# Second token blocks of an expert in whole fp32 products on 64 rows, in a hybrid decoder block on one core

## The chip, the core and the metric

The kernel runs on one core of a Trainium2 chip. The metric is the device time of one execution in microseconds. Five engines work side by side and order themselves by semaphores: TensorE (PE for its products, PEld for its weight loads), VectorE (DVE), ScalarE (ACT), GpSimd (POOL) and SyncE (SP). Transfers run on 16 DMA engines; SyncE issues most of them here, GpSimd the gathers and scatters of rows.

## The reference

One layer over 512 tokens of width 1024: a Mamba-2 mixer and a pooling mixer, merged and projected, and then a mixture of 64 experts, of which each token takes 8. Only the last part is touched by the change. In the routed experts (cut; the sorting into blocks is told in a comment):

```python
scores = jax.nn.sigmoid(uf @ w_router)            # 512 x 64
# 4 of 8 groups of experts, then the best 8 experts of these, for each token
wts = wts / jnp.sum(wts, axis=-1, keepdims=True) * ROUTED_SCALE
# the tokens of an expert, in blocks of 128:
xb = u_pad[toks]                                   # rows x 1024
hid = jax.nn.silu(xb @ we_gate[e]) * (xb @ we_up[e])   # 1024 x 256 each
y = (hid @ we_down[e]) * ws[:, None]               # 256 x 1024
# y is added to the rows of its tokens
```

An expert with up to 128 tokens has one block, one with up to 256 has two. All is float32.

## The kernel before

The mixers take about the first half of the time and the 64 experts, in a loop that is written out, the second. An expert's weights come in three tiles of 1 MB: `gu[e][0]` and `gu[e][1]` (gate and up, for one half of the 1024 inputs each) and `dn[e]`. Eight such raw tiles go round (`raw_tile`, L924); `load(e + 2)` (L1280) asks SyncE for the weights of the expert after the next, and a tile is written again when all its readers, in the code of every arm, are through.

There are two ways to compute a block.

- The heavy way splits both operands into a high and a low part of a rounded type and makes three products for each whole one (`mm3`, L59). Weights are split by ScalarE and VectorE (`split`, L43) into `wh`, `wl` or the pairs kept apart; rows are transposed by TensorE (`turn_in`), copied by ScalarE and subtracted by VectorE (`turn_out`, L902). A block of up to 128 rows takes 24 products of 512 columns for gate and up (`gate_up_mm`, L957) and 12 for the down projection (`down`, L1033).
- The light way serves experts with up to `LIGHT` = 64 tokens. It takes whole float32 products straight from the raw tiles: the gate products write partitions 0 to 63 of a PSUM tile, the up products partitions 64 to 127 (`gate_up_light`, L970), and so do the two halves of the down projection (`down_light`, L979). The products are copied out (L1185), transposed, and Silu and the multiply come after the transposes on 64 columns (L1224 to L1226).

A branch on the expert's count (`by_count`, L1155) picks one or the other at run time, on each engine by itself. Second blocks, of experts with over 128 tokens (`if_two`, L1165), always go the heavy way, on all 128 rows, though the gather and the scatter are made for 64 or 128 rows by the count (`second`, L1124). Experts with over 256 tokens are finished by a general path after the loop (`rare_blocks`, L1294), that runs if `k.rare` (L818) is set.

The order of work is written out by hand. In the turn of expert e (L1234 on) TensorE makes: the products of e (L1243); if e has a second block, its gate and up products (`second_products`); the transposes of the rows of e + 1; if e + 1 has a second block, the transposes of these rows (`next_second`); the down projection of e - 1 (`downs(e - 1)`, L1274); the transposes of the hidden rows of e (`hidden_turned`, L1275, that is L1008 with `ht`); and, if e has a second block, its hidden rows' transposes and its down projection (`second_down`, L1276). ScalarE and VectorE go through the same list with their own parts. GpSimd scatters the rows of e - 1, then those of the second block of e, and gathers for e + 2 at the start of the turn.

Second blocks use `k.xT` (the buffer of the other parity) for their rows, `hid1`, `k.hx[2]` for the hidden rows, the rows' tile `k.xg[2]` for the result, and the split weights of the first block.

Of the kernel before, what the change touches and what calls it, by code (L numbers as in the profile page):

```python
# [11 lines left out]
F32 = mybir.dt.float32  # L12
F32R = mybir.dt.float32r
BF16 = mybir.dt.bfloat16
I32 = mybir.dt.int32
AF = mybir.ActivationFunctionType
ALU = mybir.AluOpType
# [4 lines left out]
P = 128  # L22
# [734 lines left out]
def route(k, rp, lg):  # L757
# [59 lines left out]
    k.rare = mp.tile([P, 1], I32, name="rare")  # L817
    nc.vector.tensor_scalar(k.rare, cm, 2.0 * P, None, op0=ALU.is_gt)  # L818

# [98 lines left out]


def split_pair(hp, lp):  # L920
    return (hp.tile([P, 2048], F32R, name="wh", tag="wh"), lp.tile([P, 2048], F32R, name="wl", tag="wl"))
# [57 lines left out]
def down_light(k, x, unit, y, w):  # L979

    nc = k.nc
    ps = k.yo.tile([P, 512], F32, name="yo", tag="yo")
    for j in range(2):
        for n in range(2):
            nc.tensor.matmul(ps[n * LIGHT:(n + 1) * LIGHT, :], x[:, j, :], unit.raw[:, j * D + n * 512:j * D + n * 512 + 512],  # L985
                             start=j == 0, stop=j == 1)
    for n in range(2):
        nc.scalar.activation(y[:LIGHT, n * 512:(n + 1) * 512], ps[n * LIGHT:(n + 1) * LIGHT, :], AF.Copy, scale=w[:LIGHT])  # L988


# [21 lines left out]
def hidden_out(k, ps, hx):  # L1012
    nc = k.nc
    nc.scalar.copy(hx[0], ps)
    nc.vector.tensor_sub(hx[1], ps, hx[0].bitcast(F32))
# [59 lines left out]
def experts(k, shared):  # L1075
# [48 lines left out]
    def second(e, move):  # L1124
        n = count(e)
        with tc.If(n > P):
            with tc.If(n <= P + 64) as some:
                move(64)
            with some.Else():
                move(P)  # L1130

# [89 lines left out]
    def hidden_turned(e, hid):  # L1221
        ps = hidden_in(k, hid)

        def light():  # L1224
            nc.scalar.activation(k.hT, ps[:, :, :LIGHT], AF.Silu)
            nc.vector.tensor_mul(k.hT, k.hT, ps[:, :, LIGHT:])  # L1226

        by_count(e, both, light, lambda: hidden_out(k, ps, k.hx[e % 2]))

    with tc.manual_schedule():  # L1230
        fetch_over(0)
        fetch_over(1)
        if_two(0, lambda: turn(k, k.xg[3], k.xT[1]))
        for e in range(E):  # L1234
# [16 lines left out]
            def second_products():  # L1251
                gate_act(k, gate_up_mm(k, k.xT[(e + 1) % 2], gu[e]), hid1)
                turns()
# [5 lines left out]
            def next_second():  # L1259
                index_part(0)  # L1260
                turn(k, k.xg[3 + (e + 1) % 2], k.xT[e % 2])

            def second_down():
                ps = turn_tiles(k)[0].rearrange("p q t -> p (q t)")[:, :2 * P].rearrange("p (j t) -> p j t", j=2)
                hidden_in(k, hid1, ps)
                index_part(1)
                hidden_out(k, ps, k.hx[2])
                for n in range(2):
                    down(k, k.hx[2], dn[e], n, k.xg[2], idx[e][1][:, 1:2])

# [23 lines left out]
def rare_blocks(k):  # L1294
# [3 lines left out]
    with tc.If(r):  # L1298
# [4 lines left out]
        with tc.For_i(0, E, 1) as e:  # L1303
# [9 lines left out]
            split_bf16(k, k.wp, pk[:, NT:], [vv[:, :, 2 + i] for i in range(3)])  # L1313
            for b in (2, 3):
                pm = k.wp.tile([P, NT], F32, name="pmb", bufs=2)
                nc.vector.tensor_scalar(pm, pk[:, :NT], -128.0 * b, None, op0=ALU.add)
                idx = slot_rows(k, slot_onehot(k, pm, 1, nc.vector), vv, 1)
                whole_block(k, gather(k, idx, 0, k.xg[3]), idx, 0, gu, dn, k.xT[0], k.hx[0])
# [46 lines left out]
def block_kernel(ctx, tc, a, out):  # L1365
# [54 lines left out]
    with ExitStack() as p2:  # L1420
# [5 lines left out]
        k.hT = k.wp.tile([P, 2, LIGHT], F32, name="hT")  # L1426
        k.hx = [tuple(k.wp.tile([P, 2, P], F32R, name=f"h{n}{i}") for n in "hl") for i in range(3)]
        spx = ExitStack()
# [46 lines left out]
```

## Time and profile before

| | before |
|---|---|
| median of 3 runs | 1675.88 us |
| lowest and highest | 1669.54 and 1677.01 us |
| the profiled execution | 1673.0 us, its span 1671.3 us |
| granted TensorE clock, mean | 0.947 of full speed |
| busy: PE, PEld, DVE, ACT, POOL | 88%, 69%, 61%, 45%, 22% |
| moved by DMA | 340 MB, mean 204 GB/s |

The busy shares are over the whole span. The span is what lies between the first and the last instruction in the profile; the execution's time has 1.7 us around it. PE is counted busy from a product's start to its modelled end, and products overlap, so that the starts tell more than the lengths.

### The profile page before, as it was taken

What the parts mean: (1) busy time and instruction counts of PE and PEld (TensorE: products, weight loads), DVE (VectorE), ACT (ScalarE), POOL (GpSimd) and SP (SyncE); (2) the same over time, 40 slices, a digit from 0 to 9 for tenths busy, and PEclk for the clock granted to TensorE, in tenths of its full rate; (3) what the DMA queues carried; (4) which work ended last, traced back from release to release, by engine and by line L of the source; (5) the groups of instructions that cost most, each with busy time, mean ns of one, the idle gap of its engine ahead of it and who ended that gap; (6) DMA issues with size and microseconds to landing.
All of it is one profiled execution on the core that took longest, in us unless ns stands there. A gap on an engine that the chain in (4) does not pass through costs nothing. (4 is left out here: it accounts for less than half of the span.)

```text
span 1671.3 us, 25992 instructions
## 1 busy us (share of the span) xinstructions
PE 1475.4 (88%) x8084; PEld 1156.2 (69%) x8084; DVE 1011.8 (61%) x1744; ACT 745.2 (45%) x1027; POOL 370.3 (22%) x312
## 2 busy tenths in 40 slices
PE   5999999999999999999898888898798888887970
PEld 5888788788888778888675666566576665665640
DVE  6889778778877974558743354545436453355326
ACT  3465546454434223325544455444536454355332
POOL 5201101002010111220122322322324222221226
PEclk7999999999999999999999999899899989898995
DMA  9442433243333236236738778958889999898974
GB/s 288 122 126 76 138 102 121 76 126 101 107 105 117 82 114 233 87 115 227 294 113 285 252 235 289 329 189 258 282 251 313 324 329 318 287 325 273 297 288 151
DMA packets 152127, 340.32 MB, mean 204 GB/s; under 512 B 15816, under 2 KB 94832, under 8 KB 142272
## 3 DMA queue, kind: packets, MB, share of 16 engines
q1 hardware_dynamic: 135888, 294.94, 51.8%
q0 software_dynamic: 15408, 40.23, 9.4%
q8 instruction: 118, 1.93, 0.5%
q10 hardware_dynamic: 576, 2.10, 0.3%
q14 instruction: 137, 1.12, 0.2%
HBM read 314.00 MB, written 31.01 MB: 206 GB/s over the span
## 5 line engine op out<-in xcount | busy, mean ns | idle before, releaser
L46 DVE TENSOR_TENSOR wl<-raw,wh 128x2048 fp32r<-128x2048 f32 x114 | 273.5, 2404 | 100.0 <-ACT wh L45 88.4
L45 ACT CAST wh<-raw 128x2048 fp32r<-128x2048 f32 x114 | 216.6, 1906 | 140.3 <-PE mm L62 65.7
L1044 POOL DMA_INDIRECT Y<-yl,idx x64 | 108.2, 1691 | 481.8 <-ACT yl L988 271.9
L61 PE MATMUL mm<-uh,wh 128*128 128x512 f32 x432 | 171.7, 397 | 1.9 <-ACT zs L285 1.9
L63 PE MATMUL mm<-uh,wl 128*128 128x512 f32 x432 | 170.4, 395 | 0.0
L62 PE MATMUL mm<-ul,wh 128*128 128x512 f32 x432 | 169.8, 393 | 0.0
L899 PE MATMUL xt<-ident,xg 128*128 128x128 f32 x632 | 97.2, 300 | 58.2 <-issue 18.6
L899 PEld LDWEIGHTS xt<-ident,xg 128*128 128x128 f32 x632 | 84.9, 196 | 77.7 <-issue 48.9
L976 PE MATMUL gu<-raw,xf 128*64 128x256 f32 x1056 | 125.9, 387 | 6.1 <-DMA raw<-in_we_up_dram 3.5
L885 POOL DMA_INDIRECT xg<-u2d,idx x75 | 93.5, 1247 | 117.5 <-DVE oh L851 36.4
L46 DVE TENSOR_TENSOR pair<-raw,pair 128x2048 fp32r<-128x2048 f32 x33 | 75.0, 2290 | 58.2 <-ACT pair L45 49.7
L976 PEld LDWEIGHTS gu<-raw,xf 128*64 128x64 f32 x1056 | 77.2, 138 | 42.6 <-issue 7.2
L61 PE MATMUL gu<-wh,xh 128*128 128x512 f32 x256 | 103.1, 403 | 1.0 <-ACT xh L909 0.6
L62 PE MATMUL gu<-wl,xh 128*128 128x512 f32 x256 | 101.9, 398 | 0.7 <-DVEq L1169 0.7
L63 PE MATMUL gu<-wh,xl 128*128 128x512 f32 x256 | 101.3, 396 | 0.0
L1226 DVE TENSOR_TENSOR hT<-hT,ht 128x128 f32<-128x128 f32 x33 | 9.5, 288 | 146.8 <-ACTq L1169 142.5
L61 PEld LDWEIGHTS mm<-uh,wh 128*128 128x128 f32 x432 | 81.6, 189 | 20.4 <-ACT zs L285 2.3
L63 PEld LDWEIGHTS mm<-uh,wl 128*128 128x128 f32 x432 | 81.6, 189 | 17.7 <-issue 0.9
L62 PEld LDWEIGHTS mm<-ul,wh 128*128 128x128 f32 x432 | 81.5, 189 | 16.8 <-issue 0.4
L45 ACT CAST pair<-raw 128x2048 fp32r<-128x2048 f32 x33 | 62.1, 1903 | 61.7 <-DMA raw<-in_we_gate_dram 22.8
L985 PE MATMUL yo<-raw,hT 128*64 128x512 f32 x264 | 75.5, 695 | 3.5 <-DMA raw<-in_we_gate_dram 2.0
L327 DVE SCALAR_TENSOR_TENSOR cv<-mm,cw,cv 128x511 f32<-128x511 f32 (+2 forms) x90 | 66.6, 741 | 2.1 <-ACT cv L324 1.8
(354 smaller groups left out, 3336.8 us busy)
## 6 DMA issues: line engine op xcount, KB each, us to landing
raw<-in_we_gate_dram SPq DMA_DIRECT2D x124, 512.0 KB
raw<-in_we_up_dram SPq DMA_DIRECT2D x124, 512.0 KB
raw<-in_we_down_dram SPq DMA_DIRECT2D x62, 1024.0 KB
raw<-in_w_in_dram SPq DMA_DIRECT2D x27, 1024.0 KB
raw<-in_w_ada_dram SPq DMA_DIRECT2D x16, 1024.0 KB
big<-in_w_ada_dram SPq DMA_DIRECT2D x16, 512.0 KB
raw<-in_w_in_dram SPq DMA_DIRECT2D x16, 512.0 KB
raw<-in_w_br_ssd_dram SPq DMA_DIRECT2D x8, 1024.0 KB
```

The source lines that it names most:

```text
L45: nc.scalar.copy(h, raw)
L46: nc.vector.tensor_sub(l, raw, h.bitcast(F32))
L61: nc.tensor.matmul(out, sh, mh, start=first, stop=False)
L62: nc.tensor.matmul(out, sh, ml, start=False, stop=False)
L63: nc.tensor.matmul(out, sl, mh, start=False, stop=last)
L327: nc.vector.scalar_tensor_tensor(cv[:, sft:], ps[:, :T - sft], k.cw[:, j * 32 + blk:j * 32 + blk + 1], cv[:, sft:], op0=ALU.mult, op1=ALU.add)
L885: k.nc.gpsimd.indirect_dma_start(out=xg[:n], out_offset=None, in_=k.u2d, bounds_check=T - 1, oob_is_err=False, in_offset=bass.IndirectOffs ...
L899: k.nc.tensor.transpose(pv[:, q, :], xv[:, hf * 4 + q, :], k.ident)
L976: nc.tensor.matmul(ps[s * LIGHT:(s + 1) * LIGHT, :256], x[:, kk, :], w[:, s, kk % 4, :], start=kk == 0, stop=kk == NK - 1)
L985: nc.tensor.matmul(ps[n * LIGHT:(n + 1) * LIGHT, :], x[:, j, :], unit.raw[:, j * D + n * 512:j * D + n * 512 + 512], start=j == 0, stop=j ...
L1044: k.nc.gpsimd.indirect_dma_start(out=k.Y[acc], out_offset=bass.IndirectOffsetOnAxis(ap=idx[0][:n, b:b + 1], axis=0), in_=y[:n], in_offset= ...
L1226: nc.vector.tensor_mul(k.hT, k.hT, ps[:, :, LIGHT:])
```

## The change

Second blocks go the light way, on at most 64 rows: their rows are turned into `k.xf` (the light experts' tile) by copies alone (`turn_light`), gate and up are made by `gate_up_light` from the raw tiles and copied out, Silu and the multiply follow the transposes (`act_light`, which is also what light experts use now), and `down_light` writes the result with its two evictions. Gather and scatter of second blocks are always of 64 rows; the question at L1127 goes. The general path starts at over 192 tokens instead of 256, and its blocks at token 192, 320 and 448. The third pair of `k.hx` goes.

```diff
-    nc.vector.tensor_scalar(k.rare, cm, 2.0 * P, None, op0=ALU.is_gt)
+    nc.vector.tensor_scalar(k.rare, cm, float(P + LIGHT), None, op0=ALU.is_gt)
...
+def turn_light(k, src, x):
+
+    halves = turn_tiles(k)
+    turn_in(k, src, halves)
+    for hf, pv in enumerate(halves):
+        k.nc.scalar.copy(x[:, hf * 4:hf * 4 + 4, :], pv[:, :, :LIGHT])
...
+def act_light(k, ps, x):
+
+    k.nc.scalar.activation(x, ps[:, :, :LIGHT], AF.Silu)
+    k.nc.vector.tensor_mul(x, x, ps[:, :, LIGHT:])
...
     def second(e, move):
-        n = count(e)
-        with tc.If(n > P):
-            with tc.If(n <= P + 64) as some:
-                move(64)
-            with some.Else():
-                move(P)
+        with tc.If(count(e) > P):
+            move(LIGHT)
...
-        if_two(0, lambda: turn(k, k.xg[3], k.xT[1]))
+        if_two(0, lambda: turn_light(k, k.xg[3], k.xf))
...
             def second_products():
-                gate_act(k, gate_up_mm(k, k.xT[(e + 1) % 2], gu[e]), hid1)
+                g = k.gu.tile([P, 512], F32, name="gu", tag="gu")
+                gate_up_light(k, k.xf, gu[e], g)
+                nc.scalar.copy(hid1, g[:, :256])
                 turns()
...
             def next_second():
                 index_part(0)
-                turn(k, k.xg[3 + (e + 1) % 2], k.xT[e % 2])
+                turn_light(k, k.xg[3 + (e + 1) % 2], k.xf)
 
             def second_down():
                 ps = turn_tiles(k)[0].rearrange("p q t -> p (q t)")[:, :2 * P].rearrange("p (j t) -> p j t", j=2)
                 hidden_in(k, hid1, ps)
                 index_part(1)
-                hidden_out(k, ps, k.hx[2])
-                for n in range(2):
-                    down(k, k.hx[2], dn[e], n, k.xg[2], idx[e][1][:, 1:2])
+                act_light(k, ps, k.hT)
+                down_light(k, k.hT, dn[e], k.xg[2], idx[e][1][:, 1:2])
...
-            for b in (2, 3):
+            for b in range(3):
                 pm = k.wp.tile([P, NT], F32, name="pmb", bufs=2)
-                nc.vector.tensor_scalar(pm, pk[:, :NT], -128.0 * b, None, op0=ALU.add)
+                nc.vector.tensor_scalar(pm, pk[:, :NT], -float(P + LIGHT + P * b), None, op0=ALU.add)
```

## Rows read from the trace of the kernel before

**Rows 1.** The page: busy share of TensorE, and the DMA engines in 40 slices (tenths)
```profile
PE 1475.4 (88%) x8084; PEld 1156.2 (69%) x8084; DVE 1011.8 (61%) x1744; ACT 745.2 (45%) x1027; POOL 370.3 (22%) x312
DMA  9442433243333236236738778958889999898974
```

**Rows 2.** Branches by source line: TensorE's at L1169, GpSimd's at L1127 (ns: min/median/max)
```profile
L1169 PEldq COMPARE_BRANCH  x225: 65/215/2042, 808.3 to 1620.7; - x113
L1127 POOLq COMPARE_BRANCH  x44: 34/40/41, 809.2 to 1542.6; - x44
```

**Rows 3.** Gate and up products in stretches: us, PE busy (count), clock, DMA share, GB/s
```profile
902.20:916.73 14.53, 11.32 (x48) 1.00 0.73 259
934.79:949.21 14.42, 11.32 (x48) 1.00 0.83 257
...
sum 180.80, PE 124.56; mean PE 11.32
```

**Rows 4.** All of TensorE's products in the same eleven stretches, their sum
```profile
sum 180.80, PE 175.25; mean PE 15.93
```

**Rows 5.** Timeline of TensorE, 908 to 926 us: start, length, instruction, count, idle before
```profile
908.25 0.40 PE L61 MATMUL gu<-wh,xh 128*128 128x512 f32 x1
...
913.80 1.05 PE L899 MATMUL xt<-ident,xg 128*128 128x128 f32 x8
...
914.87 1.94 PE L985 MATMUL yo<-raw,hT 128*64 128x512 f32 x8
916.73 0.51 PE L1008 MATMUL ht<-ident,hid 128*128 128x128 f32 x2
...
918.96 0.51 PE L61 MATMUL yo<-pair,hh 128*128 128x512 f32 x1 [1.39 <-ACT hh L1014]
...
921.65 0.40 PE L63 MATMUL yo<-pair,hl 128*128 128x512 f32 x1
921.98 3.67 PE L976 MATMUL gu<-raw,xf 128*64 128x256 f32 x32
925.58 1.16 PE L899 MATMUL xt<-ident,xg 128*128 128x128 f32 x8
```

**Rows 6.** Timeline of ScalarE in the same stretch
```profile
903.73 0.28 ACT L1225 ACTIVATE hT<-ht 128x128 f32<-128x128 f32 x1
...
914.00 0.39 ACT L998 ACTIVATE hid<-gu 128x256 f32<-128x256 f32 x1 [5.12 <-PE gu L63]
...
916.85 1.38 ACT L988 ACTIVATE yl<-yo,wt 64x512 f32<-64x512 f32 x2 [1.53 <-PE yo L985]
...
918.52 0.38 ACT L1014 CAST hh<-xt 128x256 fp32r<-128x256 f32 x1
...
923.74 1.90 ACT L45 CAST wh<-raw 128x2048 fp32r<-128x2048 f32 x1 [0.91 <-DMA raw<-in_we_up_dram]
```

**Rows 7.** Timeline of VectorE in the same stretch
```profile
904.04 0.29 DVE L1226 TENSOR_TENSOR hT<-hT,ht 128x128 f32<-128x128 f32 x1 [3.39 <-ACTq L1169]
...
918.66 0.42 DVE L1015 TENSOR_TENSOR hl<-ht,hh 128x256 fp32r<-128x256 f32 x1 [3.82 <-ACT hh L1014]
```

**Rows 8.** ScalarE waiting for weights: a timeline row; waits from 834 to 1266 us
```profile
890.91 1.90 ACT L45 CAST wh<-raw 128x2048 fp32r<-128x2048 f32 x1 [3.54 <-DMA raw<-in_we_up_dram]
...
ACT wh L45 <- DMA raw<-in_we_up_dram: 25.3, 10, 5.4
```

**Rows 9.** Timeline of TensorE behind the fifth second block
```profile
991.89 0.48 PE L1008 MATMUL xt<-ident,hid 128*128 128x128 f32 x2 [2.66 <-DVEq L1169]
```

**Rows 10.** Timeline of SyncE's queue: the first and the last transfer of a burst
```profile
916.06 0.33 SPq L946 DMA_DIRECT2D raw<-in_we_gate_dram  x1
...
918.87 0.72 SPq L947 DMA_DIRECT2D raw<-in_we_up_dram  x1
```

**Rows 11.** Engines in the loop's two parts: PE, PEld, DVE, ACT, POOL, clock, DMA, GB/s
```profile
834.00:1266.00 432.00, 377.57 (x2147) 279.41 (x2146) 189.22 (x367) 200.46 (x283) 116.85 (x78) 0.94 0.77 248
1266.00:1628.00 362.00, 302.69 (x1819) 214.27 (x1815) 161.19 (x318) 170.17 (x241) 93.68 (x65) 0.93 0.90 308
```

More of the change, by code (lines that the diff above doesn't have):

```diff
@@ L1222, in hidden_turned @@
         ps = hidden_in(k, hid)
[L1224 to L1228, printed above, removed]
+        by_count(e, both, lambda: act_light(k, ps, k.hT), lambda: hidden_out(k, ps, k.hx[e % 2]))
     with tc.manual_schedule():
@@ L1426, in block_kernel @@
         k.hT = k.wp.tile([P, 2, LIGHT], F32, name="hT")
-        k.hx = [tuple(k.wp.tile([P, 2, P], F32R, name=f"h{n}{i}") for n in "hl") for i in range(3)]
+        k.hx = [tuple(k.wp.tile([P, 2, P], F32R, name=f"h{n}{i}") for n in "hl") for i in range(2)]
         spx = ExitStack()
```

## The prediction

> **What bounds the kernel now.** I read the page first: TensorE is busy for 88% of the span, and the transfers are lighter in the first half of the expert loop than in the second [rows 1]. Then I counted the second blocks. L1169 is every question "has this expert over 128 tokens?"; TensorE's sequencer asks it 192 times (once ahead of the loop, three times in each of 64 turns, less one in the last), and the branch out of a taken arm that has an Else is counted too: 225 - 192 = 33, three for an expert, so 11 experts have a second block. L1127 asks for each of them, once at the gather and once at the scatter, whether 192 tokens suffice: 22 questions. It stands there 44 times, so each of the 22 was followed by the branch that leaves its first arm, and no expert has over 192 tokens [rows 2]. That settles how often the changed path runs, and that the general path stays unused.
>
> For where the 11 blocks lie I cut the loop at the first transpose of an expert's hidden layer (L1008 `ht`), which gives one stretch for each expert e. The products of both blocks of e fall in its own stretch, the second block's down projection at the start of the next. In the 11 stretches the gate and up products keep TensorE busy 11.32 us on average for the two blocks, 5.66 us each [rows 3], and all TensorE work together fills 175.25 of 180.80 us [rows 4]. TensorE has no room there, so a microsecond less of its work is a microsecond less of time, unless a later wait swallows it.
>
> **The change part by part.** I take the stretch of the first block pair that is followed by a light expert, 902 to 926 us, since it shows both ways of computing side by side.
>
> *Gate and up products.* The 24 products of the second block start at 908.25 and the next work at 913.80: 5.55 us, 0.23 each. The light way is in the same view: 32 instructions from 921.98 to the next work at 925.58, 3.60 us [rows 5]. Entering the half-array form costs a little: the last full product before it starts at 921.65, so 0.33 us instead of 0.23, 0.10 more. New cost 3.70, saved 1.85 us a block, 11 x 1.85 = 20.4 us. One rule of the Trainium skill speaks against this: FP8 and Floating Point Precision, section TensorE Precision Notes, counts four passes for true fp32. By that my estimate would be 16 products x 4 x 256 columns / 2.4 GHz = 6.8 us, longer than the 5.55 of today. The row says 3.60, because the two halves (gate to partitions 0 to 63, up to 64 to 127) run side by side. The second such rule, TensorEngine Tiling (Array Packing), section Key Properties, says that changing the tiling mode drains the engine; the trace's price for that is the 0.10 us above, and it is in the sum.
>
> *What follows the products.* ScalarE's Silu and VectorE's multiply on `hid1` give way to one copy; Silu and multiply come back on 64 columns after the transposes. The first pair hid behind TensorE: ScalarE waited 5.12 us for TensorE ahead of it [rows 6]. That is also more than the 1.85 us by which TensorE now comes earlier, so ScalarE doesn't become the end here.
>
> *Turning the second block's rows.* The eight transposes stay. Two ScalarE copies of half the columns replace two copies and two VectorE subtractions. No TensorE wait ends on those subtractions in this view; I cost it at nothing. The cover is the old down projection behind it (1.86 us from 914.87 [rows 5]); it only gets wider.
>
> *Down projection.* 12 products run from 918.96 to 921.98, 3.02 us; the light form takes from 914.87 to 916.73, 1.86, and some 0.11 more for a first product after a wait (the first of the 12 has that too), 1.97 us. Saved 1.05. But the wait ahead of it grows. Today TensorE starts 0.06 us after ScalarE's second copy, at 918.52 + 0.38. In the new form that instruction is the Silu of 64 columns, 0.27 us, and then VectorE's multiply, 0.29, has to follow (904.04, right behind ScalarE's 903.73 + 0.28); VectorE is busy with the first block's subtraction from 918.66 for 0.42 [rows 5 to 7]. So the multiply starts at 919.08, ends at 919.37, and TensorE starts at 919.43, 0.47 later. Where VectorE is free it is 0.27 + 0.03 + 0.29 - 0.38 = 0.21 later. I take 0.43: the net gain is 0.62 us a block. The two evictions stay two of 0.69 (1.38 us for the pair in the light row at 916.85), but both now start after the last product, where today the first is done while the second half is computed. In this stretch ScalarE ends at 919.43 + 1.97 + 1.38 = 922.78 instead of 922.83 (0.91 before the split at 923.74 [rows 6]): nothing gained.
>
> *Which of these 0.62 us survive.* Where a light expert stands between two experts with second blocks (two of the 11), TensorE next waits for the weight split that ScalarE starts after these evictions, so the gain is nothing. Behind three others (the second, seventh and eighth of the eleven) the next heavy expert's first split waits for its weights. Behind the second it begins at 890.91, after 3.54 us of waiting, and those weights were requested in the second pair's own stretch, ahead of the down projection [rows 8]. What comes after the request and before the wait gains nothing. I drop 5 of 11 and keep 6 x 0.62 = 3.7 us. Behind the fifth pair the transposes of the second block's hidden rows already wait 2.66 us on VectorE's queue [rows 9]; I take off 0.3 us of the products' gain for that.
>
> *Weights held longer.* The second block now reads the raw tiles, not their split copies. SyncE's reloading waits for all readers of a tile, in the code of every expert. Its transfers come in bursts: the first waits for the previous expert's down projection (916.06, in TensorE's light run of 914.87), and the others follow to 918.87 [rows 10]. TensorE has passed the second block's products before that projection, so the new readers are done when the burst starts; `dn` is freed by the down projection of the first block, later still. Cost nothing; bounds zero and rival 3.
>
> *POOL, registers, general path.* The nested question at L1127 goes, 22 times some 0.04 us, on an engine that isn't at the end. The threshold in `rare` is one constant. Nothing.
>
> **Sum.** 20.4 + 3.7 - 0.3 = 23.8 us against the profiled execution: 1673.0 - 23.8 = 1649.2. That execution lies 2.9 us under the median of the runs shown, 1675.88, and inside their spread; I forecast 1650, half way to what the median would give.
>
> **The rivals.** 1, the transfers take it back. In the stretches from 834 to 1266 us, which hold ten of the pairs, the DMA engines are busy 0.77 of the time, from 1266 to 1628 us 0.90 [rows 11]. Ten pairs 2 us shorter make 0.77 of 432 into 0.81 of 412 us; on average there is room, but ScalarE already waits 25.3 us for `up` weights in the first part, ten times [rows 8]. If all of the 3.7 and 40% of the 20.4 go into such waits, 12 us stay: 1661. For it: bursts of three transfers in a row and a wait that already exists. Against: the request moves earlier with TensorE, and in the shortened stretches the share is 0.73 and 0.83 in the rows shown [rows 3].
> 2, more than the sum: no longer wait, nothing swallowed, 11 x (1.85 + 1.05) = 31.9 us, 1641. For it: VectorE loses two subtractions a block and a multiply on 256 columns. Against: VectorE's multiply is now on the way to the down products.
> 3, slower: the release of the raw tiles comes later than I read from the code, for all 64 experts. Were the second and third transfer of a burst to wait for the end of the next down projection, 921.98 instead of 916.73, they would be 5.25 us late. In the second half (31 stretches in 362 us, 11.7 each, a tenth of it without transfers) 1.2 us can be late without harm; beyond that each stretch grows, by up to 4.0 us, 31 x 4.0 = 124 us: 1773. Against it: TensorE's order above. It decides from a delay of 1.2 us, and 2 us would make the kernel slower than now (31 x 0.8 = 25).
> 4, it doesn't do what it says: the saved TensorE time is there and the ends don't move, because each stretch ends on ScalarE or VectorE splits; under 8.4 us remain. 5.5 of 180.8 us of idle time in the 11 stretches speak against it [rows 4].
>
> **How the numbers follow.** Forecast, 18 to 30 us saved: 0.60. Rival 1: 0.17. Rival 2: 0.08. Rival 4: 0.10. Rival 3, with the general path: 0.05. The range: 1638 is rival 2 less the runs' spread of 0.2%; 1664 is rival 1 plus it. It leaves out most of rivals 3 and 4, 0.15, and a little at the low end. A measurement of this kernel can tell about 0.5% from no change, 8.4 us, that is under 1667.5: faster 0.85 (forecast and rivals 1 and 2), same 0.10, slower 0.05.
>
> **What would show it.** In the trace after: L976 with 11 x 32 more instructions and the 64-column form in the 11 stretches, 3.6 to 3.7 us a block; their sum 20 us shorter; the gap ahead of the second down products at some 0.4 us longer than before (1.39 us in the row at 918.96 [rows 5]); the bursts of SyncE still starting at the previous down projection, with no wait inside. It would be wrong if the waits of ScalarE for `raw` grow by over 10 us between 834 and 1266 us, if the granted clock in the 11 stretches falls from the 1.00 that these rows show [rows 3], or if a burst is torn.

## The result

| | before | after |
|---|---|---|
| median | 1673.04 us (4 runs) | 1657.19 us (4 runs) |
| lowest and highest | 1669.54 and 1677.01 us | 1649.98 and 1660.38 us |
| ratio, with its 95% interval | | 0.9898 [0.9866, 0.9930] |
| the profiled execution, its span | 1673.0 us, 1671.3 us | 1650.0 us, 1648.3 us |

The changed kernel is faster by 1.0%, some 17 us [12 to 22]. The profiled execution of after is the fastest of its four, so that a comparison of the two traces shows 23 us, more than the medians do. I keep to what repeats in several places, and use the runs for sums.

The page of after, busy share of TensorE and the DMA engines in 40 slices, against [rows 1]: 33 us less of TensorE, and a loop that moves the same bytes in less time.

```profile
PE 1442.3 (88%) x8128; PEld 1108.5 (67%) x8128; DVE 989.8 (60%) x1711; ACT 740.4 (45%) x1027; POOL 370.4 (22%) x312
DMA  9442433342423236326758788959889999998973
```

Gate and up products in the eleven stretches (us, PE busy and count, clock, DMA share, GB/s), against [rows 3]; the stretches are those of the same experts:

```profile
893.49:906.28 12.79, 9.37 (x56) 1.00 0.89 312
927.04:939.73 12.69, 9.39 (x56) 1.00 0.94 284
...
sum 162.98, PE 103.24; mean PE 9.39
```

All of TensorE's products in the same stretches, their sum, against [rows 4]:

```profile
sum 162.98, PE 155.52; mean PE 14.14
```

The two stretches shown are 1.74 and 1.73 us shorter, all eleven together 17.8, and the DMA share in them rose from 0.73 to 0.89 and from 0.83 to 0.94. The gain isn't the same in all: seven became 1.64 to 1.79 us shorter and one 1.84; in the first, where the granted clock rose from 0.91 to 1.00, it is 3.33 us; in the sixth and the seventh, where it fell from 1.00 to 0.90 and 0.91, it is 0.21 and 0.29 us. A fall of the clock in these stretches was one of my signs of being wrong. The sixth, all of TensorE's products, before and after:

```profile
1079.95:1097.73 17.78, 15.99 (x84) 1.00 0.53 182
1069.84:1087.41 17.57, 15.82 (x93) 0.90 0.54 185
```

In the loop's two parts (all engines, then clock, DMA share, GB/s; the second part ends earlier now) the DMA engines went from 0.77 to 0.80 and from 0.90 to 0.92 [rows 11]:

```profile
834.00:1266.00 432.00, 365.32 (x2261) 249.54 (x2259) 186.92 (x362) 205.61 (x293) 120.83 (x82) 0.94 0.80 260
1266.00:1600.00 334.00, 277.03 (x1726) 192.47 (x1722) 143.64 (x291) 158.48 (x227) 88.23 (x61) 0.94 0.92 317
```

The second down projection is where the trace departs from the prediction. TensorE behind the second block pair and behind the third, which is the stretch of [rows 5]:

```profile
867.25 0.40 PE L1022 MATMUL xt<-ident,hid 128*128 128x128 f32 x2
...
869.38 1.94 PE L993 MATMUL yo<-raw,hT 128*64 128x512 f32 x8 [1.65 <-DVE hT L1002]
871.15 3.62 PE L984 MATMUL gu<-raw,xf 128*64 128x256 f32 x32
...
906.62 0.40 PE L1022 MATMUL xt<-ident,hid 128*128 128x128 f32 x2
...
909.37 3.63 PE L993 MATMUL yo<-raw,hT 128*64 128x512 f32 x8 [2.27 <-DVE hT L1002]
912.78 3.68 PE L984 MATMUL gu<-raw,xf 128*64 128x256 f32 x32
```

The wait in the stretch of [rows 5] is 2.27 us where it was 1.39, and the eight products behind it take 3.41 us to the next start (909.37 to 912.78), the same eight behind the shorter wait 1.77 (869.38 to 871.15). Two windows over these products give the reason (all engines; the clock is the third number from the end):

```profile
869.40:871.20 1.80, 1.80 (x10) 0.66 (x12) 0.00 (x0) 0.00 (x0) 0.36 (x1) 1.00 0.88 257
909.40:912.80 3.40, 3.40 (x10) 0.95 (x12) 0.00 (x0) 0.00 (x0) 0.04 (x1) 0.51 0.97 314
```

Behind 1.65 us of idling the granted clock stays at 1.00, that is 2.4 GHz; behind 2.27 us it is at 0.51, which is the lower level, 1.2 GHz. Of the eleven waits five are 1.64 or 1.65 us, all with the clock at 1.00, and six are 2.27 to 3.17 us, all with a clock of 0.52 to 0.66 behind them. ScalarE and VectorE tell why the wait is longer than planned, against [rows 6, 7]:

```profile
907.80 0.37 ACT L1028 CAST hh<-ht 128x256 fp32r<-128x256 f32 x1
908.72 0.28 ACT L1001 ACTIVATE hT<-xt 128x128 f32<-128x128 f32 x1 [0.55 <-DVE hl L1029]
```

```profile
908.21 0.42 DVE L1029 TENSOR_TENSOR hl<-ht,hh 128x256 fp32r<-128x256 f32 x1 [7.58 <-ACT hh L1028]
909.03 0.29 DVE L1002 TENSOR_TENSOR hT<-hT,xt 128x128 f32<-128x128 f32 x1 [0.40 <-issue]
```

I had put the Silu right behind ScalarE's first copy, with VectorE's subtraction beside it. In fact the Silu waits 0.55 us for that subtraction, which has nothing to do with the second block. The tile `k.hT` is written in two arms, by light experts and by second blocks, and on VectorE too (L1002). As I read it, the wait that keeps the two apart is a count of VectorE's work, and the subtraction stands in that count; the experiment with a tile of its own tests this. In ScalarE's waits between 820 and 1248 us (total, times, longest), which hold ten of the pairs, it stands ten times:

```profile
ACT wh L45 <- DMA raw<-in_we_up_dram: 19.2, 7, 6.6
...
ACT hT L1001 <- DVE hl L1029: 6.2, 10, 1.2
```

Per stretch the account is as follows. I cut both traces at the first `ht` transpose of each expert and added the lengths, worked out from these 64 starts; "next" are the nine stretches behind a second block that have none themselves (the second down projection lies there; where two second blocks follow each other, it lies in the first column), "others" the 43 that remain.

| us, from the starts | with second blocks | next | others | sum |
|---|---|---|---|---|
| before | 180.8 | 130.8 | 493.9 | 805.5 |
| after | 163.0 | 135.6 | 484.3 | 782.9 |
| difference | -17.8 | +4.8 | -9.6 | -22.6 |

The first column is the products. The second should have fallen, and rose. The third has no part in the change, and fell. Only the first repeats: in the traces of the four kernels below that have the light products too and keep the transfers (products alone, dummy products, own tile, both mends), the columns are 159.3 to 162.6, 126.2 to 129.9 and 490.1 to 494.1 us. The clock goes with the third: over the 43 others the granted clock averages 0.90 before, 0.93 in after, and 0.91, 0.91, 0.91 and 0.93 in those four. As a mix of the two levels that makes, by my estimate, 96 us at the lower one before and 65 in after; the eight products above took 3.41 us there instead of 1.77, so these 31 us can be worth up to 15. As far as related kernels can tell, most of the 9.6 us is thus this execution's own; whether the clock is the cause of the shorter stretches or follows from shorter waits isn't shown.

### The profile page after: what moved, and what is told of

Read it like the earlier page. It is cut to its first block, busy times and chain, and to the rows that moved or that the text cites. A ratio compares the mean times of both kernels' runs of the same rounds, so it can differ in the third digit from the quotient of the medians.

```text
span 1648.3 us, 25940 instructions
## 1 busy us (share of the span) xinstructions
PE 1442.3 (88%) x8128; PEld 1108.5 (67%) x8128; DVE 989.8 (60%) x1711; ACT 740.4 (45%) x1027; POOL 370.4 (22%) x312
## 5 line engine op out<-in xcount | busy, mean ns | idle before, releaser
L1058 POOL DMA_INDIRECT Y<-yl,idx x64 | 102.4, 1600 | 449.5 <-ACT yl L996 250.7
L984 PE MATMUL gu<-raw,xf 128*64 128x256 f32 x1408 | 166.8, 384 | 6.2 <-DMA raw<-in_we_up_dram 3.3
L984 PEld LDWEIGHTS gu<-raw,xf 128*64 128x64 f32 x1408 | 103.4, 138 | 61.7 <-issue 15.3
L993 PE MATMUL yo<-raw,hT 128*64 128x512 f32 x352 | 104.0, 717 | 26.7 <-DVE hT L1002 23.2
L885 POOL DMA_INDIRECT xg<-u2d,idx x75 | 99.7, 1329 | 118.1 <-DVE oh L851 36.5
L46 DVE TENSOR_TENSOR pair<-raw,pair 128x2048 fp32r<-128x2048 f32 x33 | 75.1, 2294 | 56.7 <-ACT pair L45 55.9
L1002 DVE TENSOR_TENSOR hT<-hT,ht 128x128 f32<-128x128 f32 x33 | 9.4, 286 | 150.3 <-ACTq L1179 150.3
L63 PEld LDWEIGHTS mm<-uh,wl 128*128 128x128 f32 x432 | 81.5, 189 | 17.8 <-issue 0.9
L61 PE MATMUL gu<-wh,xh 128*128 128x512 f32 x184 | 75.9, 412 | 1.0 <-ACT xh L909 0.7
L62 PE MATMUL gu<-wl,xh 128*128 128x512 f32 x184 | 74.4, 404 | 1.7 <-DVE wl L46 1.7
L63 PE MATMUL gu<-wh,xl 128*128 128x512 f32 x184 | 73.8, 401 | 0.0
L1029 DVE TENSOR_TENSOR hl<-ht,hh 128x256 fp32r<-128x256 f32 x31 | 13.1, 422 | 100.3 <-ACT hh L1028 59.7
```

What stands on the lines that cost most here:

```text
L46: nc.vector.tensor_sub(l, raw, h.bitcast(F32))
L61: nc.tensor.matmul(out, sh, mh, start=first, stop=False)
L62: nc.tensor.matmul(out, sh, ml, start=False, stop=False)
L63: nc.tensor.matmul(out, sl, mh, start=False, stop=last)
L885: k.nc.gpsimd.indirect_dma_start(out=xg[:n], out_offset=None, in_=k.u2d, bounds_check=T - 1, oob_is_err=False, in_offset=bass.IndirectOffs ...
L984: nc.tensor.matmul(ps[s * LIGHT:(s + 1) * LIGHT, :256], x[:, kk, :], w[:, s, kk % 4, :], start=kk == 0, stop=kk == NK - 1)
```

## Experiments

Two readings stood against each other at the start: that the gain is TensorE's own account, the saved products less what the down projection lost; or that the ends moved in other stretches too, for a reason of their own, and that the weight transfers cut the sum. The expectations weigh these, under letters of their own.

**The products without the light down projection.** The changed kernel with the heavy down projection for second blocks; Silu and the multiply of second blocks are left out.

```diff
-                act_light(k, ps, k.hT)
-                down_light(k, k.hT, dn[e], k.xg[2], idx[e][1][:, 1:2])
+                hidden_out(k, ps, k.hx[2])
+                for n in range(2):
+                    down(k, k.hx[2], dn[e], n, k.xg[2], idx[e][1][:, 1:2])
```

> The kernel after, with the second block's down projection put back to the heavy form (12 products, hidden rows split); Silu and the multiply of the second block are left out, since they have no place between the two forms, and are not in the output. Theory A (the light products save what TensorE had to spare nothing of, and the down projection gave part of it back): the second block's gate and up products take 3.6 us instead of 5.55, the time falls by 11 x 1.75 = 19 us, ratio 0.988. Rival B (the transfers swallow part of the products' gain): at most 12 us less, 0.993 or above, with longer waits of ScalarE for weights.

Measured: 1652.27 us, 0.9873 [0.9838, 0.9908]. The light products without the light down projection give all that the whole change gives, within the intervals.

**The light down projection alone.** The kernel before, whose second blocks end in one ScalarE copy of 64 columns, into a tile of its own, and `down_light`.

```diff
-                hidden_out(k, ps, k.hx[2])
-                for n in range(2):
-                    down(k, k.hx[2], dn[e], n, k.xg[2], idx[e][1][:, 1:2])
+                nc.scalar.copy(k.hT2, ps[:, :, :LIGHT])
+                down_light(k, k.hT2, dn[e], k.xg[2], idx[e][1][:, 1:2])
```

> The kernel before, with the second block's down projection alone in the light form, from a tile of its own that ScalarE fills by one copy (VectorE not on the way). Theory A (the light down projection is cheap in itself, the loss lay in the longer wait ahead of it and in the clock that falls in it): wait at most as long as before (0.8 to 1.4 us), 8 instructions in 1.8 to 1.9 us at a granted clock of 1.00, saving 11 x 1.2 = 13 us, ratio 0.992. Rival C (half-array products lose the clock or drain the array by themselves): down projections of 2.5 us and more at a clock under 0.7 though the wait is short, ratio 0.997 or above.

Measured: 1670.08 us, 0.9984 [0.9958, 1.0009], no change that can be told. TensorE had what I wanted from the step: from the second block's hidden transposes to the next products the eleven blocks take 36.3 us instead of 49.7. Ten of them make their products in 1.77 to 1.87 us at a clock of 1.00; the fifth takes 3.61 us at 0.50, behind a wait of 2.66 us ahead of its hidden transposes and one of 0.32 us behind them. One place shows where some of the 13.4 us go, the two stretches behind the fourth block pair (TensorE busy and count, clock, DMA share, GB/s), first of before, then of this kernel:

```profile
949.21:961.99 12.78, 11.39 (x78) 1.00 0.92 308
961.99:974.16 12.17, 10.05 (x67) 0.86 0.94 279
```

```profile
946.60:957.98 11.38, 10.09 (x75) 1.00 0.93 306
957.98:971.08 13.10, 9.86 (x68) 0.89 1.00 310
```

The stretch with the down projection is 1.40 us shorter, the one behind it 0.93 us longer, and its DMA share is 1.00. In the account above the nine "next" stretches fall by 9.0 us (130.8 to 121.8) and the 43 others rise by 7.6 (493.9 to 501.5; their clock is 0.89).

**Dummy products in the wait.** After, with 16 more transposes of the identity between the hidden transposes and the second down projection; nothing reads them.

```diff
+                for i in range(16):
+                    nc.tensor.transpose(two[1][:, i % 4, :], k.ident, k.ident)
```

> The kernel after, with 16 transposes of a constant into an unused buffer while TensorE waits for the second block's hidden rows. Theory A (the granted clock fell in six of the eleven down projections because TensorE stood idle 2.3 us and more ahead of them): the wait in time stays, the clock stays at 1.00, these six take 1.8 us instead of 2.7 to 3.5, together some 8 us less than the kernel after, ratio to before 0.985. Rival C (the clock falls for another reason, the half-array products or the transfers): it falls as before, ratio as that of the kernel after, 0.990, or above by the added work.

Measured: 1650.40 us, 0.9853 [0.9817, 0.9888]. From the hidden transposes to the down products it takes 2.75 us as in after, with 0.47 us of waiting left, and the down products run at the full clock. TensorE in the stretch of [rows 5]:

```profile
908.54 1.95 PE L1277 MATMUL xt<-ident 128*128 128x128 f32 x16
910.95 1.94 PE L993 MATMUL yo<-raw,hT 128*64 128x512 f32 x8 [0.47 <-issue]
```

All eleven take 1.77 to 1.87 us now, at a clock of 1.00, where six took 2.67 to 3.48. So the length of those six was the clock's and not a cost of the half-array form. The whole from hidden transposes to next products falls from 56.4 to 48.6 us. In the kernel's time this can't be told: the interval overlaps that of after, 0.9866 to 0.9930.

**A tile of its own.** After, with `k.hT2` for second blocks.

```diff
-                act_light(k, ps, k.hT)
-                down_light(k, k.hT, dn[e], k.xg[2], idx[e][1][:, 1:2])
+                act_light(k, ps, k.hT2)
+                down_light(k, k.hT2, dn[e], k.xg[2], idx[e][1][:, 1:2])
```

> The kernel after, with a tile of its own for the second block's hidden rows instead of the light experts' tile. Theory A (ScalarE's Silu waits for VectorE's subtraction of the first block only because both arms share one tile): the 0.3 to 1.2 us by which ScalarE waits for that subtraction go, the wait ahead of the down products shrinks by about 0.5 us in each of 11 blocks, 5 us, and by up to 5 us more where the clock then stays up; ratio to before 0.984 to 0.987. Rival D (the longer wait is VectorE's multiply alone, as I had forecast): the wait stays, ratio 0.990.

Measured: 1651.64 us, 0.9860 [0.9827, 0.9892]. The waits of 1.64 us became 1.14, those of 2.27 became 1.77, 0.50 less each: the shared tile is the cause of that half microsecond. What is left over the 0.76 and 1.39 of before is 0.38, and the prediction had 0.43. Here too the interval of the whole time overlaps that of after. The clock does not follow the wait's length alone. Two waits of 1.77 us, the third and the fourth block pair:

```profile
912.84 3.38 PE L993 MATMUL yo<-raw,hTs 128*64 128x512 f32 x8 [1.77 <-DVE hTs L1002]
...
944.22 1.94 PE L993 MATMUL yo<-raw,hTs 128*64 128x512 f32 x8 [1.77 <-DVE hTs L1002]
```

```profile
912.90:916.00 3.10, 3.10 (x9) 0.55 0.91 251
944.20:945.90 1.70, 1.68 (x8) 1.00 0.92 246
```

**Without the weights' transfers.** Both kernels, with the experts' weights not loaded from the fifth expert on; what is computed with them is left out with them. Everything else runs as before, on old contents of the raw tiles.

```diff
             gu[e], dn[e] = [Unit(k), Unit(k)], Unit(k)
-            with tc.If(count(e, (ET.SP,)) > 0):
-                load_gu(k, a.we_gate[0, e], a.we_up[0, e], gu[e])
-                load_down(k, a.we_down[0, e], dn[e])
```

> The kernel before without the weight transfers of the experts from the fifth on: these use whatever weights the earlier ones left in the eight raw tiles, so the routed part of the output is not the reference's. It is the base for the next two. Every theory: the waits of ScalarE for weights go, some 70 us of the time with them, ratio 0.95 to 0.96.

> The kernel after, with the same weight transfers left out. Theory A (the products save 11 x 1.75 = 19 us of TensorE, the down projections lose 7, and with no transfer to hide either, both show in full): 12 us less than the kernel before without the transfers. Rival E (the loss in the down projections is swallowed by work of ScalarE and VectorE, not by transfers): 17 to 19 us less, as with the transfers.

Measured: 1591.66 us (0.9508 [0.9487, 0.9529]) and 1557.78 us (0.9301 [0.9282, 0.9321]). The change is worth 33.9 us here, twice what it gives with the transfers, and more than either theory expected. By stretches: 182.1 to 161.4 with second blocks, 130.8 to 130.6 next, 413.2 to 397.7 in the others.

**The light down projection alone, without transfers.** The second experiment again.

> The kernel before with the down projection alone in the light form, with the same weight transfers left out. With the transfers TensorE's part of the second down projections was 13.4 us shorter and the time 3 us. Theory W (the next heavy expert's weights, requested ahead of the down projection, swallow the rest): without the transfers 10 to 13 us less than the kernel before without them. Rival E (ScalarE's evictions, which end no earlier than before, swallow it): again 3 us, up to 5.

Measured: 1574.99 us, 0.9414 [0.9394, 0.9434], 16.7 us less than 1591.66; with the transfers the same edit gave 3. Here the others don't give the gain back: they fall by 4.6 us instead of rising by 7.6.

**VectorE's part alone.** Without the transfers the others fell by 15.5 us without a product of theirs being changed, so something had made room there. In the kernel before, VectorE has four instructions in the arms of second blocks, in after one. This is the kernel before with its three subtractions left out (the rows' two and the hidden rows' one); the high parts stand in for the low ones, so that TensorE makes the same 36 products.

```diff
-                turn(k, k.xg[3 + (e + 1) % 2], k.xT[e % 2])
+                turn_copies(k, k.xg[3 + (e + 1) % 2], k.xT[e % 2][0])
...
-                hidden_out(k, ps, k.hx[2])
+                nc.scalar.copy(k.hx[2], ps)
                 for n in range(2):
-                    down(k, k.hx[2], dn[e], n, k.xg[2], idx[e][1][:, 1:2])
+                    down(k, (k.hx[2],) * 2, dn[e], n, k.xg[2], idx[e][1][:, 1:2])
```

> The kernel before, with VectorE's three subtractions of a second block left out (two for the rows, one for the hidden rows); the high parts stand in for the low ones, so that TensorE makes the same 36 products as before and the result lacks the low parts. Theory V (VectorE's work in the arms of second blocks is what the stretches without a saving of TensorE gained): 6 to 12 us faster than before, since the transfers take about half of what the same edit gives without them. Theory N (those stretches gained only because TensorE was early): within 3 us of before.

> The same without the transfers of the experts' weights from the fifth expert on (what is computed with them is left out with them). The kernel before without transfers takes 1591.7 us, the changed one 1557.8, and 20.7 us of the 34 lie in the stretches with second blocks. Theory V: 10 to 20 us faster than 1591.7, with shorter heavy stretches (0.4 to 1.2 us each) though TensorE's products are the same. Theory N: 1588 to 1592.

Measured: 1667.46 us with transfers, 0.9955 [0.9939, 0.9972], 7.5 us by that ratio; 1579.37 us without (0.9433 [0.9410, 0.9456]), 12.3 us less than 1591.66. Both are what theory V expected. Where the gain lies only the trace without transfers shows: the next stretches fall by 4.2 us and the others by 9.6. With transfers the profiled execution (1672.0 us) is above the median of its runs, and its loop is 804.7 us where that of before is 805.5.

Experts 32 to 54 have no second block among them. Without transfers their 23 stretches are 6.5 us shorter here than in the kernel before, 6.2 in after and 6.3 with both mends (below), so that this part repeats. By the estimate above the clock makes at most 1.7 us of it (10 us at the lower level before, 7 in each of the three). The others up to expert 30 fell by 3.5 us here, 4.7 with both mends and 9.8 in after, and there the clock differs, as the last experiment shows. With transfers the 23 stretches moved by -5.8 to +1.6 us in the six kernels that have the light products or lack the subtractions: no gain that can be told.

The instructions of the question "over 128 tokens?" on VectorE, without transfers, before and then with the subtractions out (ns, min/median/max):

```profile
L1166 DVEq EVENT_SEMAPHORE  x159: 21/21/21, 811.5 to 1545.1; - x159
```

```profile
L1173 DVEq EVENT_SEMAPHORE  x53: 21/21/21, 815.3 to 1526.5; - x53
```

The semaphore steps of arms not taken went from 159 to 53, as many as in after. 106 steps of 21 ns are 2.2 us, so the steps alone don't make it. The stretch of expert 33, which has no second block and lies between two heavy experts, shows what hangs on it; VectorE and TensorE, first before, then with the subtractions out, both without transfers:

```profile
1255.36 0.42 DVE L1015 TENSOR_TENSOR hl<-ht,hh 128x256 fp32r<-128x256 f32 x1 [0.60 <-ACT wh L45]
...
1261.53 0.41 DVE L999 TENSOR_TENSOR hid<-hid,gu 128x256 f32<-128x256 f32 x1
...
1262.09 0.48 PE L1008 MATMUL ht<-ident,hid 128*128 128x128 f32 x2 [0.63 <-DVEq L1166]
```

```profile
1248.42 0.42 DVE L1022 TENSOR_TENSOR hl<-ht,hh 128x256 fp32r<-128x256 f32 x1
...
1254.28 0.41 DVE L1006 TENSOR_TENSOR hid<-hid,gu 128x256 f32<-128x256 f32 x1
...
1255.03 0.39 PE L1015 MATMUL ht<-ident,hid 128*128 128x128 f32 x2
```

Here, between two heavy experts, VectorE sets the pace. Before, it passes from one hidden subtraction to the multiply of the next in 6.17 us (1255.36 to 1261.53), with a wait of 0.60 ahead, and TensorE's hidden transposes wait 0.63 us for its queue; with the subtractions out it is 5.86 us, without those waits, and this stretch is 0.81 us shorter. That such stretches shorten when only arms that they don't take are emptied is shown. Whether it is the waits that the steps sit in, those of other engines for the subtractions, or the place that they give to VectorE's next instruction isn't taken apart here. ScalarE's part of the change (copies of half the columns, a copy in place of the first Silu) has no experiment of its own.

**Both hidden transposes early.** After, with a tile of its own and the hidden transposes of both blocks ahead of the down projection of e - 1, so that this projection covers the wait; the hidden rows of experts without a second block are turned in the other arm of the second question.

```diff
-            downs(e - 1)
-            hidden_turned(e, hid)
-            if_two(e, second_down, lambda: index_part(1))
+            both_ps = hidden_tile(k)
+            if_two(e, both_hidden)
+            downs(e - 1)
+            if_two(e, second_down, one_down)
```

> The kernel after with a tile of its own for the second block's hidden rows, and with the hidden rows of both blocks transposed and worked on ahead of the previous expert's down projection, which then covers the wait (PSUM tile of the hidden rows twice as large). Theory A: no wait ahead of the second down products, clock 1.00 in them, TensorE's part of the eleven falls from 50 to under 30 us. By theory W the weights swallow three quarters of that: ratio to before 0.980 to 0.986. Rival E or no swallowing: 0.975 or below.

Measured: 1704.32 us, 1.0184 [1.0152, 1.0216]: 31 us slower than before where I expected it faster. TensorE's waits from about 800 us on (total, times, longest), of after and of this kernel:

```profile
PE ht L1022 <- DVEq L1170: 16.1, 6, 6.9
```

```profile
PE ht L1026 <- DVEq L1183: 59.3, 16, 8.6
```

The hidden transposes wait 59.3 us for VectorE's queue at the second question, and none of the sixteen stands at an expert with a second block (four of them lie from 1266 to 1305 us, between heavy experts). In the stretches that it was made for the wait ahead of the second down projection did shrink, from 2.27 to 1.29 us in that of [rows 5], and ends on ScalarE's evictions now:

```profile
915.97 1.94 PE L993 MATMUL yo<-raw,hTs 128*64 128x512 f32 x8 [1.29 <-ACT yl L996]
```

As I read it, this is the same dependence from its bad side: work moved into an arm makes every expert wait for VectorE at that question. The rows point there; I haven't isolated it. The PSUM tile of the hidden rows, now shared by both blocks, is another possible cause, also untested.

**Both mends.** After, with the tile of its own and the dummy transposes, with and without transfers.

> The changed kernel with both mends of the second down projection: a tile of its own for the second block's hidden rows, and 16 dummy transposes in the wait. Alone they gave 0.986 and 0.985 of before. If the wait and the clock add up, TensorE's time from the second block's hidden transposes to the end of its down projection falls from 56.4 us in the changed kernel to some 42, and the ratio is 0.980 to 0.985, 1640 to 1648 us. If the transfers take back what TensorE gains, as they did with the light down projection alone, it stays at 0.984 to 0.988, 1648 to 1655 us.

> The changed kernel with both mends of the second down projection (own tile, dummy transposes), without the transfers of the experts' weights from the fifth expert on; what is computed with them is left out with them. The mends took 10.8 us of TensorE's time out of the second down projections and gave nothing that was measured against the changed kernel's own ratio. If the transfers swallow it, it appears without them: 8 to 12 us under the 1557.8 us of the changed kernel without transfers, 1546 to 1550. If another engine takes it (ScalarE's evictions or VectorE's chain of the next block), it stays at 1554 to 1558.

Measured: 1650.30 us, 0.9870 [0.9848, 0.9892]; without transfers 1553.59 us, 0.9263 [0.9226, 0.9300]. From hidden transposes to next products TensorE needs 45.6 us in both instead of 56.4 and 56.8, but both intervals overlap those of after (0.9898 [0.9866, 0.9930], and 0.9301 [0.9282, 0.9321] without transfers). Without them I expected 8 to 12 us and saw 4.2: the "next" stretches fell by 7.1 us (130.6 to 123.5), and the others rose by 4.4 (397.7 to 402.1) although none of their work was touched. One of them, expert 5's, after and then with the mends, both without transfers:

```profile
885.72 1.40 PE L899 MATMUL xt<-ident,xg 128*128 128x128 f32 x8 [1.89 <-issue]
887.04 1.94 PE L993 MATMUL yo<-raw,hT 128*64 128x512 f32 x8
```

```profile
886.27 1.83 PE L899 MATMUL xt<-ident,xg 128*128 128x128 f32 x8 [1.89 <-issue]
888.03 2.85 PE L993 MATMUL yo<-raw,hT 128*64 128x512 f32 x8
```

and the clock over these rows:

```profile
885.70:888.90 3.20, 3.18 (x16) 1.00 0.10 31
```

```profile
886.20:890.80 4.60, 4.53 (x16) 0.63 0.09 26
```

The same instructions behind the same wait of 1.89 us ran at 1.00 in one kernel and at 0.63 in the other. Six stretches of this kind (experts 1, 5, 10 and 19 among the others, 20 with a second block, 29 a next one) are 1.4 to 1.9 us longer with the mends, 9.3 us together. Their granted clock is 0.85 to 0.90 with the mends and 0.86 to 0.92 in the kernel before without transfers, but 1.00 in after. So some of the 33.9 us between the two kernels without transfers is this, too. The five executions of after without transfers lie between 1555.75 and 1558.56 us, so it doesn't look like the luck of one; but no run shows what in the change would bring it about.

## Why the prediction came out as it did

The forecast was 1650 us, that is 24 us saved against the profiled execution of before; the runs give some 17 [12 to 22], inside the range, but short of the 18 to 30 us that had most of the chance and above the 12 us of rival 1. The sum was near by terms that were not all right.

**The products: right.** 3.6 us a block, as the row of the light expert had it, and eleven times. The seven stretches that TensorE fills from end to end became 1.64 to 1.79 us shorter, where I had 1.85, so that eleven make some 19 us. The eleven together are 17.8 us with the transfers and 20.7 without, against 20.4, but these sums hold falls and rises of the clock like those of the first and the sixth stretch. The rule of four passes for true fp32 in the Trainium skill (FP8 and Floating Point Precision, TensorE Precision Notes) made the block longer only because I counted the 16 products in a row. With the eight of each half side by side my estimate from it is 8 x 4 x 256 columns / 2.4 GHz = 3.4 us, and the trace's 3.60 us agrees.

**The down projection: wrong in sign.** I had the wait ahead of it 0.43 us longer and 0.62 us gained. The wait grew by 0.88 us in eight blocks (0.76 to 1.64 in five, 1.39 to 2.27 in three), by more in the others, and in six blocks the clock fell and took another 0.9 to 1.6 us (before, it had fallen in one, the fifth). From hidden transposes to next products: 49.7 us before, 56.4 after, 6.7 lost where I had 11 x 0.62 = 6.8 won and 3.7 of it in the sum. The step that failed is "so the multiply starts at 919.08": I let ScalarE's Silu follow its own copy at once. With a tile of its own the wait grows by 0.38 us, which is the step as I had written it. What I hadn't read was that `act_light(k, ps, k.hT)` puts two arms on one tile, and that a wait for it is a wait in VectorE's order. A fall of the clock I had named for the eleven stretches alone, without a price; here, where I was lengthening waits of up to 1.39 us, I left it out.

Most of the 6.7 us is a wait that changed its place. Ahead of the hidden transposes of the fifth and the eleventh second block TensorE waited 2.66 [rows 9] and 2.65 us before; after, that is 0.12 and 0.17. The eleventh, before and after:

```profile
1537.75 0.48 PE L1008 MATMUL xt<-ident,hid 128*128 128x128 f32 x2 [2.65 <-DVEq L1169]
1509.86 0.51 PE L1022 MATMUL xt<-ident,hid 128*128 128x128 f32 x2 [0.17 <-ACTq L1179]
```

With these waits the eleven blocks take 55.0 us before and 56.7 after: 1.7 us lost, and still none of the 6.8 won.

**Behind the fifth pair** I took off 0.3 us. The 2.66 us of [rows 9] are gone there; instead the second down products wait 3.17, because VectorE starts a split of 2.28 us ahead of the subtraction:

```profile
978.33 2.28 DVE L46 TENSOR_TENSOR wl<-raw,wh 128x2048 fp32r<-128x2048 f32 x1
980.53 0.41 DVE L1029 TENSOR_TENSOR hl<-ht,hh 128x256 fp32r<-128x256 f32 x1
981.35 0.29 DVE L1002 TENSOR_TENSOR hT<-hT,xt 128x128 f32<-128x128 f32 x1 [0.40 <-ACT hT L1001]
```

**Turning the rows: "I cost it at nothing" was too low.** I looked for a TensorE wait on the second block's subtractions, in one stretch, and found none. With the subtraction of the hidden rows they are worth 7.5 us with transfers and 12.3 without; of the latter some 6 lie in stretches far from any second block, where VectorE steps over them. In the rivals I gave VectorE's relief as a reason for rival 2, and then weighed only its place ahead of the down products.

**Which gains survive: the idea was right, its place too narrow.** I dropped 5 of 11 gains of the down projection for the transfers and let those of the products stand. The pairs of runs with and without transfers measure it for whole edits: 16.7 against 3 us for the light down projection, 12.3 against 7.5 for VectorE's relief, 33.9 against some 17 for the change. So rival 1 is true in kind, for edits as wholes. In the stretches with second blocks little of it shows: their gain is 17.8 to 21.5 us in the five kernels with light products and transfers, and 20.7 without transfers. The price of 1661 that I gave it was too high by 4 us; as I read it, because VectorE's gain stood against it.

**Weights held longer: right.** The burst of SyncE that answers [rows 10] is whole, 2.93 us from first to last start where it was 2.81, and rival 3 didn't come about:

```profile
905.60 0.33 SPq L954 DMA_DIRECT2D raw<-in_we_gate_dram  x1
...
908.53 0.80 SPq L955 DMA_DIRECT2D raw<-in_we_up_dram  x1
```

ScalarE's wait for `up` weights ahead of `wh`, 25.3 us in [rows 8], is 19.2 in the row shown above, over the same experts. All its waits for `raw` together rose: 36.0 us before between 834 and 1266 us, 45.5 after, just short of the rise of 10 us that I had named (39.7 over the same experts). Rival 4 falls with the eleven stretches.

So the account as the runs have it, without transfers: the two profiled executions differ by 20.7 us in the stretches with second blocks, by 0.2 in the next ones, where the down projection lies, and by 15.5 in the others. Of these 15.5 us some 6 are VectorE's in arms not taken, and some 6 more go with a clock that is 1.00 in after, but 0.85 to 0.91 before and with both mends; the rest isn't taken apart. With the transfers about half of the whole is left, 17 of 33.9 us. That the total is near the forecast is partly luck: VectorE's part, put at nothing, stood against a down projection with the wrong sign and against what the transfers took.

## What to carry to other kernels

Before a chain between engines is priced by durations, look at the tiles that it writes: one that another arm of a branch writes too brings the waits of that arm's readers with it, in the order of their queue. What an engine does in an arm that is seldom taken can cost in every pass, so look for the gain of emptying it where the arm is not taken. And measure an edit once with the transfers taken away: where the two differ, the transfers hold the difference. Before a shorter stretch that the change doesn't touch is called its effect, compare the granted clock there, and see whether it repeats in a related kernel.

## What the runs showed of the hardware

- The granted clock behind a wait of TensorE: ahead of the second down projections all five waits of 1.64 or 1.65 us in after left it at 1.00, and all six of 2.27 us or more were followed by 0.52 to 0.66. That isn't a rule for all places: in the kernel before, 2.66 and 2.65 us ahead of the hidden transposes, with 0.43 and 0.42 us behind them, were followed by 0.65 once and by 1.00 once. In between it goes both ways, too: 1.77 us gave 1.00 once and 0.55 or 0.56 three times in one execution, and 1.89 us gave 1.00 in one kernel and 0.63 in another. The Trainium skill, TensorE: Matmul & The Clock Gate, section What's actually happening, says that what the gate counts by runs free of the kernel's own start, so that the point of a change varies; the two rows of 1.89 us agree with that, as far as one pair can.
- Sixteen dummy transposes in a wait held the clock at 1.00 in all eleven places, and the down products behind them took 1.77 to 1.87 us instead of up to 3.48. The kernel's time didn't move beyond its interval.
- A question on the token count cost VectorE 43 to 72 ns in its branch, and 21 ns for each semaphore step of an arm not taken; yet leaving three instructions out of such arms, which eleven experts take and 53 step over, moved the whole kernel by 7.5 us with transfers and 12.3 without. Some 6 of the 12.3 lie among 23 stretches that step over them.
